# Subtractions moved to VectorE, sums moved into PSUM, gathers and small matmuls issued in another order, in a two-block kernel

## The chip, the cores and the metric

One core of one Trainium2 chip. The metric is device time in microseconds (us), the median of several executions; one more execution was recorded by the hardware profiler, and its views are quoted here. The engines are named as in the profile: PE (TensorE matmul) and PEld (its weight loads), DVE (VectorE), ACT (ScalarE), POOL (GpSimd), SP (SyncE, which here issues most DMAs).

## The reference

512 tokens of width 1024 pass through two blocks. What matters here, cut down:

```
# block 1: attention heads and a 31-tap depthwise convolution side by side
h = a * sigmoid(gate);  h = depthwise_conv(h, 31 taps) + b;  silu(layernorm(h))
# then PEER: 8 heads x 16 experts of 16384 per token
q = x @ wq;  top-k of two halves -> e (expert numbers), g (softmax weights)
h = gelu(x . u[e]);   y = sum_k g*h * v[e]
# block 2: RWKV-7 and NSA attention side by side, gated mix, conv FFN
z = z + (prev - z) * mu                # token shift, prev = z one token earlier
state = state*w + (state@a) b + v k    # 16 heads of 64, in chunks
```

## The kernel before

**Products.** PE multiplies in a fast format that keeps fewer bits, so each matrix is split into a high part (a cast on ACT) and a low part (raw minus high, a subtraction), and each product is three matmuls: hi·hi, lo·hi, hi·lo (`mm3`, L258, recorded at L264 to L266). `Stream` (L208) does that for weights: SP loads a raw tile `wr`, ACT casts `wh` (L245), and POOL subtracts `wl` (L247), or VectorE for the tile numbers in `dve`; for the expert stream `uT` these are tiles 12 to 57.

**Block 1.** `phase1` computes the projections tile by tile, four tiles of convolution channels and attention. `taps` (L346) adds 26 of the 31 taps on VectorE, all but the first with a scalar_tensor_tensor from SBUF tiles into an SBUF accumulator (L353); five are summed on ACT and POOL into `side`, and L355 adds the two. Attention scores go to PSUM banks `pb`, their values to one of two banks `po` for two heads at a time, and `mm` (two banks) takes the projections.

**PEER.** The first 384 tokens are done densely: all 128 tiles of 128 experts (`up`: L821, product with the weights at L832, split at L834 and L835; PE's second product at L861). Of these tiles, 68 are computed ahead, while selection runs (`ahead`), and their `gh` are kept in DRAM. The weights come from one-hot matrices made on VectorE (L774, L777) and multiplied on PE (L782). The last 128 tokens are done by gathers: for each of 128 slots POOL issues an indirect DMA (L796) of the experts' rows `ur` and later `vr`; VectorE reduces `ur` (L805, `slot_up`) and adds `vr` times the result into `acc` (L813, `slot_down`). `v_split` (L673) splits the v tile of each expert tile in halves, of which POOL subtracts one and VectorE the other (L683). The loop from L850 on does one expert tile, one reduction and one update per step; VectorE's and POOL's instructions of a step stand in one queue each.

**Block 2.** `shifted` (L1022) takes a projection from PSUM, multiplies it by the row factors into `z` (L1028), subtracts it from the token before (L1029) and adds `mu` times that (L1030). `Rwkv.pair` (L1481) multiplies the two 64-row halves of a tile on PE (L1486), four column pieces of one half after the other; `front.lower` (L1597) does the same for the chunk matrices (L1603); `invert` works with 32x32 pieces (L1546, L1551, L1553).

**Order.** The engines run their queues in order. A scheduler in the kernel's builder places the instructions of each engine by its own simulation of the program, under the program's dependences and buffer counts; so code that is moved or given to another engine reorders its surroundings too.

## Time and profile before

| | us |
|---|---|
| median of 3 runs (2991.15 to 3003.77) | 2994.53 |
| profiled execution, device time | 2995.58 |
| its span in the profile | 2993.8 |
| busy PE, PEld | 2812.0, 2395.3 |
| busy DVE, ACT, POOL | 2242.7, 1203.3, 1644.9 |

The profile is of one execution. Busy times are unions of an engine's instructions; a line's mean is its mean duration, which for an in-order engine contains the time in which an instruction that has started is held up. "Idle before" is the time in which the engine had nothing running before that group, with what ended it. PE records two instructions for each fp32 matmul. The stages of the span are: up to 300 us block 1's first half, to 773 selection and the tiles ahead, to 1600 the expert loop, to 1930 RWKV's preparation, to 2250 its chunks, then NSA, mixing and FFN.

### The profile page before, as it was taken

What the parts mean: (1) busy time and instruction counts of PE and PEld (TensorE: products, weight loads), DVE (VectorE), ACT (ScalarE), POOL (GpSimd) and SP (SyncE); (2) the same over time, 40 slices, a digit from 0 to 9 for tenths busy, and PEclk for the clock granted to TensorE, in tenths of its full rate; (3) what the DMA queues carried; (4) which work ended last, traced back from release to release, by engine and by line L of the source; (5) the groups of instructions that cost most, each with busy time, mean ns of one, the idle gap of its engine ahead of it and who ended that gap; (6) DMA issues with size and microseconds to landing.
All of it is one profiled execution on the core that took longest, in us unless ns stands there. A gap on an engine that the chain in (4) does not pass through costs nothing. (4 is left out here: it accounts for less than half of the span.)

```text
span 2993.8 us, 42580 instructions
## 1 busy us (share of the span) xinstructions
PE 2812.0 (94%) x15507; PEld 2395.3 (80%) x15507; DVE 2242.7 (75%) x3813; ACT 1203.3 (40%) x2077; POOL 1644.9 (55%) x1157
## 2 busy tenths in 40 slices
PE   7789999998899999999997998999999999999998
PEld 5558899997788888888875786788887877888887
DVE  7984899987689999999996598886336874575611
ACT  4344335676233333333433432211236754444431
POOL 5543340003778888888883476523347745554444
PEclk8779999999999999999998999989999999999999
DMA  3101235676989999999974555544743227233332
GB/s 133 42 15 45 85 120 175 210 275 252 340 304 341 335 331 344 340 324 333 331 277 125 182 165 151 161 145 142 203 143 101 75 64 244 89 99 93 97 93 77
DMA packets 270919, 554.02 MB, mean 185 GB/s; under 512 B 41394, under 2 KB 147890, under 8 KB 268916
## 3 DMA queue, kind: packets, MB, share of 16 engines
q1 hardware_dynamic: 219264, 370.91, 38.5%
q0 software_dynamic: 36864, 134.23, 12.3%
q10 hardware_dynamic: 14580, 46.15, 4.3%
q8 instruction: 122, 2.00, 0.3%
q14 instruction: 89, 0.73, 0.1%
HBM read 464.77 MB, written 83.89 MB: 183 GB/s over the span
## 5 line engine op out<-in xcount | busy, mean ns | idle before, releaser
L247 POOL TENSOR_TENSOR wl<-wr,wh 128x1024 fp32r<-128x1024 f32 x273 | 695.6, 2550 | 538.0 <-ACT wh L245 254.0
L245 ACT CAST wh<-wr 128x1024 fp32r<-128x1024 f32 x319 | 335.3, 1051 | 607.3 <-PE mm L265 163.1
L683 POOL TENSOR_TENSOR vl<-vr,vh 128x512 fp32r<-128x512 f32 x128 | 200.9, 1575 | 244.9 <-ACT vh L682 243.5
L805 DVE CUSTOM_DVE_ANT_0 ur<-ur,hnt 128x1024 f32<-128x1024 f32 x128 | 231.5, 1809 | 44.0 <-DMA ur<-in_u,eix 42.8
L813 DVE SCALAR_TENSOR_TENSOR acc<-vr,hc,acc 128x1024 f32<-128x1024 f32 x128 | 232.5, 1816 | 0.2
L796 POOL DMA_INDIRECT ur<-in_u,eix x128 | 176.6, 1379 | 42.2 <-issue 16.3
L796 POOL DMA_INDIRECT vr<-in_vrow,eix x128 | 156.8, 1225 | 40.3 <-issue 22.1
L861 PE MATMUL pb<-vl,ah 128*128 128x512 f32 x512 | 168.7, 400 | 0.0
L861 PE MATMUL pb<-vh,al 128*128 128x512 f32 x512 | 165.1, 396 | 0.0
L683 DVE TENSOR_TENSOR vl<-vr,vh 128x512 fp32r<-128x512 f32 x128 | 143.7, 1129 | 27.3 <-issue 14.4
L861 PE MATMUL pb<-vh,ah 128*128 128x512 f32 x512 | 162.8, 398 | 0.0
L682 ACT CAST vh<-vr 128x512 fp32r<-128x512 f32 x256 | 144.3, 619 | 31.4 <-DMA vr<-in_vrow 21.3
L353 DVE SCALAR_TENSOR_TENSOR acc<-hp,vecs,acc 128x512 f32<-128x512 f32 x100 | 116.0, 1175 | 0.7
L861 PEld LDWEIGHTS pb<-vl,ah 128*128 128x128 f32 x512 | 97.7, 191 | 23.1
L861 PEld LDWEIGHTS pb<-vh,ah 128*128 128x128 f32 x512 | 97.7, 191 | 22.3
L861 PEld LDWEIGHTS pb<-vh,al 128*128 128x128 f32 x512 | 97.3, 190 | 22.8
L785 ACT ACTIVATE wb<-pb 128x512 f32<-128x512 f32 x96 | 98.2, 1151 | 34.4 <-PE pb L782 33.4
L1944 POOL TENSOR_TENSOR prob<-prob,nz 128x128 f32<-128x128 f32 (+3 forms) x128 | 88.8, 725 | 39.4 <-DVE nz L1941 24.0
L1169 DVE TENSOR_TENSOR tot<-tot,sq 128x512 f32<-128x512 f32 x11 | 17.0, 1548 | 112.9 <-ACT sq L1166 112.9
L861 PE MATMUL po<-vl,ah 128*128 128x512 f32 x256 | 86.5, 402 | 12.2 <-POOL vl L683 8.1
L861 PE MATMUL po<-vh,ah 128*128 128x512 f32 x256 | 85.1, 399 | 12.4 <-ACT ah L834 12.4
L861 PE MATMUL po<-vh,al 128*128 128x512 f32 x256 | 86.3, 402 | 0.0
(1407 smaller groups left out, 8788.4 us busy)
## 6 DMA issues: line engine op xcount, KB each, us to landing
wr<-in_ws SPq DMA_DIRECT2D x191, 512.0 KB
wr<-in_uT SPq DMA_DIRECT2D x128, 512.0 KB
vr<-in_vrow SPq DMA_DIRECT2D x128, 512.0 KB
w_d<-wb ACTq DMA_DIRECT2D x12, 2048.0 KB
wt<-w_d SPq DMA_DIRECT2D x32, 768.0 KB
gh_d<-gh ACTq DMA_DIRECT2D x68, 192.0 KB
gh<-gh_d SPq DMA_DIRECT2D x68, 192.0 KB
rd_d<-z SPq DMA_DIRECT2D x24, 256.0 KB
```

The lines of the kernel that those rows point to most:

```text
L245: c.nc.scalar.copy(h, r)
L247: eng.tensor_sub(lo, r, h)
L353: nc.vector.scalar_tensor_tensor(acc[j], hp[:, tap:tap + S], w[:, tap:tap + 1], acc[j], op0=OP.mult, op1=OP.add)
L682: nc.scalar.copy(h[:, s], r[:, s])
L683: (nc.vector if e % 2 else nc.gpsimd).tensor_sub(lo[:, s], r[:, s], h[:, s])
L785: nc.scalar.activation(wb[:, :, t4:t4 + 4].rearrange("p e t -> p t e"), wp.rearrange("p (t e) -> p t e", t=4), AF.Copy, scale=1.0 / GSCALE)
L796: nc.gpsimd.indirect_dma_start(out=t, out_offset=None, in_=src, in_offset=bass.IndirectOffsetOnAxis(ap=eix[:, s:s + 1], axis=0))
L805: nc.vector.tensor_tensor_reduce(out=u, in0=u, in1=hnt, scale=1.0, scalar=0.0, op0=OP.mult, op1=OP.add, accum_out=hc[:, s:s + 1])
L813: nc.vector.scalar_tensor_tensor(acc, v, ghs[gi][:, s:s + 1], acc, op0=OP.mult, op1=OP.add)
L861: nc.tensor.matmul(outs[i][half], ps[a][:, ts], vs[v][:, half * 512:(half + 1) * 512], start=et == 0 and n == 0, stop=et == NE - 1 and n == 2)
L1169: nc.vector.tensor_add(tot, tot, sq)
L1944: nc.gpsimd.tensor_mul(t, t, z[:, i:i + 1].to_broadcast([P, (i + 1) * P]))
```

## The change

Five edits:

1. `taps` accumulates in a PSUM bank of `po` and writes the SBUF accumulator only in the last addition.
2. `shifted` scales `z` by `1 - mu` on ACT into the projection's own PSUM bank, and one VectorE operation adds `mu` times the token before. The factors `own` are made once.
3. All `v_split` subtractions and all of the `uT` stream from tile 12 on go to VectorE.
4. The first four gathers are issued where the v tiles of the loop's start are split, ahead of the last token tile's one-hots; the reductions of group 0 follow after all tiles ahead; in the loop, the reduction follows `up` as before, from another place in the code.
5. Small matmuls on 64 rows (`pair`, `lower`) and on 32x32 pieces (`invert`) go in turn to two row groups and two banks.

```diff
-                nc.vector.scalar_tensor_tensor(acc[j], hp[:, tap:tap + S], w[:, tap:tap + 1], acc[j], op0=OP.mult, op1=OP.add)
+                nc.vector.scalar_tensor_tensor(ps, hp[:, tap:tap + S], w[:, tap:tap + 1], ps, op0=OP.mult, op1=OP.add)
...
-            nc.vector.tensor_add(acc[j], acc[j], sides[j])
+            nc.vector.tensor_add(acc[j], ps, sides[j])
...
-            (nc.vector if e % 2 else nc.gpsimd).tensor_sub(lo[:, s], r[:, s], h[:, s])
+            nc.vector.tensor_sub(lo[:, s], r[:, s], h[:, s])
...
+            u0 = [gather(c.ins["u"], s, "ur") for s in range(SG)]
...
-        u = gather(c.ins["u"], gi * SG + s, "ur")
+        u = u0[s] if gi == 0 else gather(c.ins["u"], gi * SG + s, "ur")
...
-        slot_up(gi, e)
...
     ahead(NB)
+    for s in range(SG):
+        slot_up(0, s)
...
                 up(gi + 1, e, wts[gi + 1])
+                slot_up(gi + 1, e)
...
-        nc.vector.tensor_mul(z[:, 1:], early.pop(0) if early else proj(), rs)
-        nc.vector.tensor_sub(o, z[:, 0:S], z[:, 1:])
-        nc.vector.scalar_tensor_tensor(o, o, c.vec("mu", n), z[:, 1:], op0=OP.mult, op1=OP.add)
+        ps = early.pop(0) if early else proj()
+        nc.vector.tensor_mul(z[:, 1:], ps, rs)
+
+        nc.scalar.activation(ps, z[:, 1:], AF.Copy, scale=own[:, n:n + 1])
+        nc.vector.scalar_tensor_tensor(o, z[:, 0:S], c.vec("mu", n), ps, op0=OP.mult, op1=OP.add)
...
-            for par in range(2):
-                rows = slice(par * 64, par * 64 + 64)
-                ps = self.bank()
-                for j in range(4):
+            pss = [self.bank() for _ in range(2)]
+            for j in range(4):
+                for par, ps in enumerate(pss):
+                    rows = slice(par * 64, par * 64 + 64)
                     nc.tensor.matmul(ps[:, j * P:(j + 1) * P], lhs[rows, j], rhs[rows, j], start=True, stop=True)
...
-                peer(c, st, Stream(c, [ins["uT"][k] for k in pre_tiles()], dve=range(NTOP, NTOP + NROUTE)), last)
+                peer(c, st, Stream(c, [ins["uT"][k] for k in pre_tiles()], dve=range(NTOP, NE)), last)
```

How the order moves, at three places. First VectorE's queue at the end of the convolution, before (`acc_194` is the fourth channel's accumulator, `mx` and `zs` are softmax maxima and sums):

```order
L435 TENSOR_REDUCE mx_1298<-pb_1294 128x1
L436 TENSOR_TENSOR mx_1274<-mx_1274,hr_1083 128x1
L436 TENSOR_TENSOR mx_1286<-mx_1286,hr_1083 128x1
L353 SCALAR_TENSOR_TENSOR acc_194<-hp_912,vecs,acc_194 128x512
L282 TENSOR_TENSOR hsl_1255<-hn_1236,hsh_1254 128x512
L436 TENSOR_TENSOR mx_1298<-mx_1298,hr_1083 128x1
L439 RECIPROCAL zs_1263<-zs_1263 128x1
L353 SCALAR_TENSOR_TENSOR acc_194<-hp_912,vecs,acc_194 128x512
L439 RECIPROCAL zs_1275<-zs_1275 128x1
L439 RECIPROCAL zs_1287<-zs_1287 128x1
L355 TENSOR_TENSOR acc_194<-acc_194,side_916 128x512
L439 RECIPROCAL zs_1299<-zs_1299 128x1
```

And after (`po_1312` and `po_1392` are the banks of the third and fourth channel; more such rows in turn stand ahead of these):

```order
L355 SCALAR_TENSOR_TENSOR po_1392<-hp_913,vecs,po_1392 128x512
L355 SCALAR_TENSOR_TENSOR po_1312<-hp_666,vecs,po_1312 128x512
L355 SCALAR_TENSOR_TENSOR po_1392<-hp_913,vecs,po_1392 128x512
L357 TENSOR_TENSOR acc_193<-po_1312,side_670 128x512
L355 SCALAR_TENSOR_TENSOR po_1392<-hp_913,vecs,po_1392 128x512 x15
L357 TENSOR_TENSOR acc_194<-po_1392,side_917 128x512
L495 SCALAR_TENSOR_TENSOR acc_191<-mm_1420,acc_191 128x512
L495 SCALAR_TENSOR_TENSOR acc_192<-mm_1420,acc_192 128x512
```

The taps of the last two channels stood among the attention's operations; now some 35 stand together, and the last channel's begin only once the bank of the second pair of heads is read. PE's matmuls on `acc_193` and `acc_194` follow in its queue right behind the last scores.

Second, POOL's queue where the expert loop begins, before (`wl` are weight splits, `ur` and `vr` gathers):

```order
L247 TENSOR_TENSOR wl_7509<-wr_7444,wh_7508 128x1024
L845 MEMSET acc 128x1024
L247 TENSOR_TENSOR wl_7543<-wr_7478,wh_7542 128x1024
L247 TENSOR_TENSOR wl_7577<-wr_7512,wh_7576 128x1024
L247 TENSOR_TENSOR wl_7611<-wr_7546,wh_7610 128x1024
L796 DMA ur_7655<-in_u,eix 128x1024
L796 DMA ur_7665<-in_u,eix 128x1024
L796 DMA ur_7675<-in_u,eix 128x1024
L796 DMA ur_7685<-in_u,eix 128x1024
```

and after:

```order
L248 TENSOR_TENSOR wl_3878<-wr_3813,wh_3877 128x1024
L248 TENSOR_TENSOR wl_3912<-wr_3847,wh_3911 128x1024
L690 DMA ur_6500<-in_u,eix 128x1024
L690 DMA ur_6502<-in_u,eix 128x1024
L690 DMA ur_6504<-in_u,eix 128x1024
L690 DMA ur_6506<-in_u,eix 128x1024
L849 MEMSET acc 128x1024
L690 DMA ur_7715<-in_u,eix 128x1024
L690 DMA vr_7744<-in_vrow,eix 128x1024
L690 DMA ur_7754<-in_u,eix 128x1024
```

The gathers (L690 after, since the helper is moved) stood behind the splits of the last tiles ahead and then in turn with `vl` and `wl` subtractions; now four stand ahead of the clearing of `acc`, and behind it gathers only.

Third, PE's queue at the first of `pair`'s matmuls, before (`kk` and `a` are its operands, `xg` and `wh`, `wl` a projection's):

```order
L265 MATMUL mm_15765<-xg6l,wh_15644 128x512
L266 MATMUL mm_15765<-xg6h,wl_15645 128x512
L1486 MATMUL pb_15352<-kk_15289,a_15286 128x128 x4
L1486 MATMUL pb_15358<-kk_15289,a_15286 128x128 x4
L1443 MATMUL pb_15489<-sqm,tmp_15486 128x2 x4
L264 MATMUL mm_15765<-xg7h,wh_15644 128x512
```

and after (six of the eight, which alternate between two banks):

```order
L266 MATMUL mm_15649<-xg6l,wh_15613 128x512
L267 MATMUL mm_15649<-xg6h,wl_15614 128x512
L1496 MATMUL pb_15358<-kk_15295,a_15292 128x128
L1496 MATMUL pb_15359<-kk_15295,a_15292 128x128
L1496 MATMUL pb_15358<-kk_15295,a_15292 128x128
L1496 MATMUL pb_15359<-kk_15295,a_15292 128x128
L1496 MATMUL pb_15358<-kk_15295,a_15292 128x128
L1496 MATMUL pb_15359<-kk_15295,a_15292 128x128
```

Of the 192 matmuls in `lower` 110 stand singly between matmuls of the other bank; 82 still come in runs of two to four in the same bank. Of `invert`'s 128 at L1546, 64 stand in turn.

## Rows read from the trace of the kernel before

**Rows 1.** The page: busy us (share of the span) xinstructions, whole run.

```profile
PE 2812.0 (94%) x15507; PEld 2395.3 (80%) x15507; DVE 2242.7 (75%) x3813; ACT 1203.3 (40%) x2077; POOL 1644.9 (55%) x1157
```

**Rows 2.** Table by stage: start:end, length, busy us by engine, granted clock, DMA share, GB/s.

```profile
52.00:206.00 154.00, 119.44 (x427) 84.56 (x427) 146.86 (x204) 61.03 (x108) 84.62 (x49) 0.77 0.10 31
...
850.00:1500.00 650.00, 645.72 (x3081) 562.07 (x3080) 611.24 (x638) 233.02 (x438) 557.79 (x354) 1.00 0.94 332
1700.00:1930.00 230.00, 211.58 (x1141) 172.82 (x1142) 209.28 (x238) 63.33 (x108) 156.74 (x103) 0.95 0.53 154
1930.00:2250.00 320.00, 310.27 (x2599) 271.87 (x2598) 171.38 (x341) 71.78 (x123) 120.34 (x103) 0.94 0.52 159
```

**Rows 3.** Groups by line, VectorE, 52 to 206 us: busy us, mean ns, idle before.

```profile
L353 DVE SCALAR_TENSOR_TENSOR acc<-hp,vecs,acc 128x512 f32<-128x512 f32 x92 | 103.3, 1139 | 0.5
L435 DVE TENSOR_REDUCE mx<-pb 128x1 f32<-128x512 f32 x20 | 13.4, 678 | 4.7 <-PE pb L433 4.7
```

**Rows 4.** Timeline, 75 us: start, duration, engine and line.

```profile
74.92 2.59 POOL L247 TENSOR_TENSOR wl<-wr,wh 128x1024 fp32r<-128x1024 f32 x1 [4.24 <-ACT wh L245]
...
75.28 2.77 DVE L355 TENSOR_TENSOR acc<-acc,side 128x512 f32<-128x512 f32 x1
```

**Rows 5.** What PE waited for, 660 to 780 us: total, times, longest.

```profile
PE pb L782 <- DVE og L777: 11.6, 8, 3.3
```

**Rows 6.** One-hots on VectorE: the group, 660 to 730 us.

```profile
L777 DVE TENSOR_TENSOR og<-o,gs 128x1024 f16<-128x1024 f16 x32 | 28.4, 922 | 0.6 <-PE pb L782 0.4
```

**Rows 7.** The same, timeline, 704 us.

```profile
703.93 1.28 DVE L777 TENSOR_TENSOR og<-o,gs 128x1024 f16<-128x1024 f16 x2
```

**Rows 8.** Groups by line, VectorE, whole run: weight splits while POOL rests.

```profile
L247 DVE TENSOR_TENSOR wl<-wr,wh 128x1024 fp32r<-128x1024 f32 x46 | 55.8, 1214 | 9.1 <-ACT wh L245 8.9
```

**Rows 9.** Timeline, 766 to 783 us, POOL's gathers and VectorE.

```profile
766.61 0.94 POOL L796 DMA_INDIRECT ur<-in_u,eix  x1 [0.30 <-issue]
...
770.93 1.23 DVE L805 CUSTOM_DVE_ANT_0 ur<-ur,hnt 128x1024 f32<-128x1024 f32 x1 [41.50 <-DMA ur<-in_u,eix]
...
778.74 1.28 DVE L813 SCALAR_TENSOR_TENSOR acc<-vr,hc,acc 128x1024 f32<-128x1024 f32 x1
...
783.22 1.84 POOL L796 DMA_INDIRECT ur<-in_u,eix  x1 [0.31 <-DVE al L835]
```

**Rows 10.** What PE waited for, 780 to 1600 us.

```profile
PE po L861 <- ACT ah L834: 12.4, 3, 8.0
PE po L861 <- POOL vl L683: 8.1, 11, 2.3
```

**Rows 11.** Groups by line and form, VectorE, 850 to 1500 us.

```profile
L805 DVE CUSTOM_DVE_ANT_0 ur<-ur,hnt 128x1024 f32<-128x1024 f32 x101 | 187.3, 1855 | 1.0 <-DMA ur<-in_u,eix 1.0
L813 DVE SCALAR_TENSOR_TENSOR acc<-vr,hc,acc 128x1024 f32<-128x1024 f32 x102 | 184.3, 1807 | 0.0
L683 DVE TENSOR_TENSOR vl<-vr,vh 128x512 fp32r<-128x512 f32 x101 | 116.4, 1157 | 17.8 <-issue 13.3 <-ACT vh L682 4.3
...
L832 DVE TENSOR_TENSOR mm<-mm,wt 128x384 f32<-128x384 f32 x52 | 28.8, 554 | 4.7 <-ACT mm L830 4.7
```

**Rows 12.** Groups by line, VectorE, 1690 to 1960 us: the token shift.

```profile
L1030 DVE SCALAR_TENSOR_TENSOR z<-z,vecs,z 128x512 f32<-128x512 f32 x20 | 29.3, 1465 | 0.3
L1029 DVE TENSOR_TENSOR z<-z 128x512 f32<-128x512 f32 x20 | 24.5, 1226 | 13.7 <-POOL z L1027 12.8
```

**Rows 13.** Groups by line, PE, 1700 to 2260 us: the small matmuls.

```profile
L1603 PE MATMUL pb<-ar,ck 64*128 64x128 f32 x384 | 51.0, 300 | 0.7 <-ACT X L1617 0.6
...
L1486 PE MATMUL pb<-kk,a 64*128 64x128 f32 x128 | 14.1, 289 | 3.2 <-DVE kk L1480 3.2
...
L1546 PE MATMUL po<-c4y,LT 32*32 32x32 f32 x256 | 9.9, 193 | 0.0
```

**Rows 14.** Timeline, 2050 us: the first and the sixth of a series.

```profile
2049.82 0.19 PE L1553 MATMUL po<-c4y,zz 32*32 32x32 f32 x1
...
2049.90 0.19 PE L1551 MATMUL po<-zz,c4y 32*32 32x32 f32 x1
```

More of the change, by code (lines that the diff above doesn't have):

```diff
@@ L88 @@
 DEC = math.exp(-0.5)
+NMU = 27
 def _tables2():
@@ L349, in taps @@
         for j in range(4):
-            w, hp = c.vec("cdw", j * 31, 31), conv[j]
-            nc.vector.tensor_scalar(acc[j], hp[:, SIDE:SIDE + S], w[:, SIDE:SIDE + 1], None, op0=OP.mult)
+            w, hp, ps = c.vec("cdw", j * 31, 31), conv[j], c.bank("po", 2)
+            nc.vector.tensor_scalar(ps, hp[:, SIDE:SIDE + S], w[:, SIDE:SIDE + 1], None, op0=OP.mult)
             for tap in range(SIDE + 1, 31):
-                nc.vector.scalar_tensor_tensor(acc[j], hp[:, tap:tap + S], w[:, tap:tap + 1], acc[j], op0=OP.mult, op1=OP.add)
+                nc.vector.scalar_tensor_tensor(ps, hp[:, tap:tap + S], w[:, tap:tap + 1], ps, op0=OP.mult, op1=OP.add)
                 yield
-            nc.vector.tensor_add(acc[j], acc[j], sides[j])
+            nc.vector.tensor_add(acc[j], ps, sides[j])
             yield
@@ L544 @@
 NSEL = 4
-NROUTE = NT * NSEL + ND * 10
 TB = 32
@@ L682, in v_split, with gather @@
             nc.scalar.copy(h[:, s], r[:, s])
-            (nc.vector if e % 2 else nc.gpsimd).tensor_sub(lo[:, s], r[:, s], h[:, s])
+            nc.vector.tensor_sub(lo[:, s], r[:, s], h[:, s])
         vsplit[et] = (h, lo)
         v_load(et + VRAW)
+    def gather(src, s, tag):
+        t = c.t4(tag)
+        nc.gpsimd.indirect_dma_start(out=t, out_offset=None, in_=src,
+                                     in_offset=bass.IndirectOffsetOnAxis(ap=eix[:, s:s + 1], axis=0))
+        return t
     for i in order:
@@ L792, in peer @@
     nc.sync.dma_start(hnt, hnt_d)
-    def gather(src, s, tag):
-        t = c.t4(tag)
-        nc.gpsimd.indirect_dma_start(out=t, out_offset=None, in_=src,
-                                     in_offset=bass.IndirectOffsetOnAxis(ap=eix[:, s:s + 1], axis=0))
-        return t
     def slot_up(gi, s):
@@ L1020, in block2 @@
     ntile = [0]
+    own = c.sb.tile([P, NMU], F32, name="own", tag="own", bufs=1)
+    nc.vector.tensor_scalar(own, c.vec("mu", 0, NMU), -1.0, 1.0, op0=OP.mult, op1=OP.add)
     def shifted(o):
@@ L1480, in pair @@
         nc.vector.scalar_tensor_tensor(kk, kk, -1.0, e3, op0=OP.mult, op1=OP.mult)
-        for par in range(2):
-            rows = slice(par * 64, par * 64 + 64)
-            ps = self.bank()
-            for n in range(4):
-                cs = slice(n * P, (n + 1) * P)
+        pss = [self.bank() for _ in range(2)]
+        for n in range(4):
+            cs = slice(n * P, (n + 1) * P)
+            for par, ps in enumerate(pss):
+                rows = slice(par * 64, par * 64 + 64)
                 nc.tensor.matmul(ps[:, cs], a[rows, cs], kk[rows, cs], start=True, stop=True)
+        for par, ps in enumerate(pss):
             nc.vector.tensor_mul(self.LT[g][:, :, par * 4 + j], ps.rearrange("p (n t) -> p n t", n=4),
@@ L1542, in invert @@
                 st.append((u0, pt, q64, c.bank("po", 2), self.sm("zz", [P, 8, 32], bufs=2)))
-            for q0, q1 in quads:
-                for u0, pt, q64, z1, zz in st:
-                    for u in range(8):
+            turns = [[(quads[(a + b) % 2], st[a]) for a in range(2)] for b in range(2)]
+            for turn in turns:
+                for u in range(8):
+                    for (q0, q1), (u0, pt, q64, z1, zz) in turn:
                         nc.tensor.matmul(z1[q1, u * 32:(u + 1) * 32], pt[q0, u, q1], Qc[q0, u0 + u, :], start=True, stop=True)
+                for (q0, q1), (u0, pt, q64, z1, zz) in turn:
                     nc.vector.tensor_copy(zz[q1], z1[q1, 0:256].rearrange("p (u i) -> p u i", u=8))
-            for q0, q1 in quads:
-                for u0, pt, q64, z1, zz in st:
-                    for u in range(8):
+            for turn in turns:
+                for u in range(8):
+                    for (q0, q1), (u0, pt, q64, z1, zz) in turn:
                         nc.tensor.matmul(z1[q1, 256 + u * 32:256 + (u + 1) * 32], Pc[q1, u0 + u, :], zz[q1, u, :],
                                          start=True, stop=True)
+                    for (q0, q1), (u0, pt, q64, z1, zz) in turn:
                         nc.tensor.matmul(z1[q0, 256 + u * 32:256 + (u + 1) * 32], zz[q1, u, :], Pc[q1, u0 + u, :],
                                          start=True, stop=True)
+                for (q0, q1), (u0, pt, q64, z1, zz) in turn:
                     nc.vector.tensor_copy(q64[q1, :, 0:32], z1[q1, 256:512].rearrange("p (u i) -> p u i", u=8))
@@ L1598, in lower @@
             r = []
-            for par in range(2):
-                rows = slice(par * 64, par * 64 + 64)
-                ps = self.bank()
-                for j in range(4):
+            pss = [self.bank() for _ in range(2)]
+            for j in range(4):
+                for par, ps in enumerate(pss):
+                    rows = slice(par * 64, par * 64 + 64)
                     nc.tensor.matmul(ps[:, j * P:(j + 1) * P], lhs[rows, j], rhs[rows, j], start=True, stop=True)
+            for ps in pss:
                 t = self.sm(tag, [P, 4, P], 4 if tag == "rb" else 2)
```

## The prediction

> **What bounds the kernel now.** I read the busy table of the page first. TensorE (PE) is busy for 2812.0 of 2993.8 us, so there are some 180 us in which it does nothing, and whatever the change frees on another engine can be worth only the part of these that it touches [rows 1]. The second view is the table by stage, since the whole-run share hides four different limits. The reader is to see there that in 52 to 206 us (projections, convolution, first attention heads) VectorE is busy for 146.86 of 154 us and PE for 119.44; that the expert loop (850 to 1500) belongs to PE with 645.72 of 650; that in 1700 to 1930 (RWKV preparation) both PE and VectorE are over nine tenths full; and that 1930 to 2250 (RWKV chunks) is PE's with 310.27 of 320 [rows 2]. Third, groups of instructions by line, for what VectorE pays; fourth, the timeline where a duration looks odd; last, what PE waited for.
>
> VectorE's price depends on what GpSimd (POOL) does. A tap takes 1139 ns on average in 52 to 206, although a VectorE operation of the same width that reads PSUM takes 678 [rows 3]. The timeline shows where it comes from: a POOL subtraction starts at 74.92 and runs 2.59 us, and the VectorE addition of two SBUF tiles issued at 75.28 ends with it, after 2.77 us [rows 4]. So three parts of the change attack one thing: two-input SBUF work on VectorE held by POOL arithmetic.
>
> **The change part by part** (against the profiled execution's 2995.58 us; the median of the runs shown is 2994.53, 1 us less).
>
> *Taps into PSUM.* 92 taps lie in the stretch. At 0.68 instead of 1.139 us VectorE gets back 92 x 0.46 = 42 us [rows 3]. PE can use at most its idle 154 - 119 = 35 us [rows 2]. But the order says that not all comes: attention and taps now share the two `po` banks, so the second channel waits while the first scores are done with no tap between, and the last channel can start only when the second pair of heads has left its bank. The last 35 taps stand almost in one piece, with PE's next matmul (the convolution's mean) needing their sum: 35 x 0.68 = 24 us in which PE has nothing, where before the last taps lay between scores. 42 - 24 = 18; attention's own chain is likely to take a third of it, and I take **-12**. Bounds: -35 (PE's idle time gone) and +24 (the tail comes on top of everything as it was).
>
> *Last one-hots.* From 660 to 780 PE waited 11.6 us for the weighted one-hots [rows 5]. The 32 of them take 922 ns each, two undisturbed ones 1.28 us, so POOL holds them for 32 x 0.28 = 9 us, and more on the plain one-hots beside them [rows 6, 7]. With four gathers on POOL there and fewer subtractions, that mostly goes. Against it stand more weight splits on VectorE of 1.21 us each [rows 8], most of them after 730, where VectorE sits idle for 41.5 us [rows 9]. **-6**; bounds -12 and +5.
>
> *Loop start, loop and tail.* From 780 to 1600 PE waited 12.4 us for `ah`, in three waits with one of 8.0, and 8.1 us for `vl` from POOL [rows 10]. The 8.0 us is a queue: the gathers were being issued at 766, behind POOL's subtractions, VectorE idled 41.50 us for the first of them, then had five reductions to do before the products that make `ah` [rows 9]. After, the four gathers are issued before the last one-hots, and POOL holds no subtraction at all, so both waits go: 20 us. What becomes late next is VectorE, which now does all subtractions. Per slot, at undisturbed durations: reduction 1.23 and update 1.28 [rows 9], two `vl` subtractions of half a 1.21 each [rows 8], product and split of the activations 0.55 each, and half a `wl` subtraction (52 of 102 slots compute their projection here) 0.6 [rows 11]: 5.4 us. PE needs 650 / 102 = 6.37 us a slot [rows 2, 11]. The loop stays PE's, with nearly 1 us to spare, and its pace does not change. **-20**; bounds -25 and, if the spare is not there, the slower case below.
>
> The disturbance that is left is the gather itself: its issue takes POOL 0.94 us with VectorE idle and 1.84 us beside VectorE's products [rows 9]. The Trainium skill (page "SBUF — State Buffer", the "DVE blocks DMA" box in "SBUF: two separate sides") warns that VectorE's two-port operations starve the descriptors that GpSimd writes, and its section "Who interferes with whom" infers that tensor_tensor does not; the 1.84 us shows that something is shared here after all. By the warning a denser VectorE would make gathers late. Two of 1.84 are 3.7 us of POOL's 6.37 us slot, so by the rows it stays hidden, and I leave it a part of the slower case.
>
> *Token shift.* 20 of 24 tiles lie in 1690 to 1960: 1226 + 1465 ns for the pair of operations [rows 12]; one with a PSUM input at 0.68 replaces them: 20 x 2.0 = 40 us less on VectorE, out of 209.28 in 230. PE has only 230 - 211.58 = 18 us idle there [rows 2]. ScalarE takes the new scaling (63 of 230 us busy). The `mm` bank is held longer, through multiply, copy and last operation, which often stand side by side in VectorE's queue, so that VectorE waits there for ScalarE, about as long as one PSUM operation. The next projection has the second bank. Of 18 us I take 7. The paired matmuls of this stage (L1486, 14.1 us [rows 13]) now alternate row halves; halved they give 7. **-14**; bounds -25 and +5 (the waits for ScalarE and for the bank eat it all).
>
> *Row halves in the chunks.* L1603 is busy for 51.0 us in 384 records, two to a matmul [rows 13]. In the order after, 110 of its 192 matmuls stand alternately; the others still come in runs, as the scheduler left them. Halving 57% of 51.0 gives 15; half of the 32x32 ones of L1546 (9.9 us) alternate too and give 2. Three quarters of 17, since PE is full there but sits in chains: **-13**. No row shows two row halves side by side; the bounds are 0 and -25. The nearest row: the 32x32 matmuls of L1551 and L1553, which alternate column halves in the same rows, start about 16 ns apart [rows 14], against 9.9 us / 256 = 39 ns for L1546, which stays in one place [rows 13].
>
> The Trainium skill (page "TensorE: Matmul & The Clock Gate", Part 3 "Packing small matmuls") says that a weight load overlaps a running matmul only where the row group differs. By that the alternation would at least halve these matmuls, and L1551 with L1553 should go no faster than L1546; rows 14 shows that they do, so column halves overlap as well and the rule is not the whole story. By the rule alone the two terms would be the same as mine, with the bound of nothing ruled out.
>
> Sum: -12 - 6 - 20 - 14 - 13 = -65, 2930.6 by the profiled execution and **2930** by the median's level. NSA, mixing and FFN keep their order and their time.
>
> **Rivals.**
> 1. *All of it converts.* -35 - 12 - 25 - 25 - 25 = -122: 2873. For it: every wait named is real idle time of PE. Against it: the tail of taps and the small idle time of the RWKV stages.
> 2. *Only the queues' waits go.* Row halves give nothing (+13 + 7 against the forecast) and the taps' tail eats the convolution's gain (+12): 2962. For it: the shared `po` banks, no row of overlapping halves.
> 3. *No change to be measured.* The tail of taps costs its full 24 us instead of gaining 12 (+36) and the row halves give nothing (+20): 2986.
> 4. *Slower: VectorE becomes the loop's bound.* If gathers hold it as the subtractions did, its slot costs what before's contended means say: 1.855 + 1.807 + 2 x 1.157 [rows 11] + 1.1 + 0.6 = 7.7 us; 1.32 us over PE's 6.37 in 124 slots is +164, less the 45 that the other parts give: about 3114. It decides from 6.37 + 45 / 124 = 6.73 us a slot. Against it: reduction and update take 1.23 and 1.28 us at loop start, between gathers [rows 9]; for it: VectorE's queue is in order, and one late gather now holds up all the splits behind it.
>
> **How the numbers follow.** Forecast 0.50 (2905 to 2955), rival 1 0.15, rival 2 0.20, rival 3 0.08, rival 4 0.07. A measurement of this kernel can tell about 0.5%, 15 us, from no change. Faster: 0.50 + 0.15 + 0.20 = 0.85; same 0.08; slower 0.07. The range 2875 to 2975 takes in the forecast, most of rival 2 and half of rival 1, and leaves out some 2 in 10.
>
> **What would show it.** The taps and the last operation of the shift at about 0.68 us, with a block of taps at the end of the convolution in which PE idles some 20 us; no wait of 8 us for `ah` at the loop's start; reduction and update near 1.25 us in the loop and VectorE under 6 us a slot; L1603 well under 51 us. Wrong it would be if the reduction stays near 1.8 us without subtractions on POOL (something else holds VectorE), if PE's share of the loop falls under 0.98, if L1603 keeps its 51 us, or if PE waits for the `mm` bank at each shifted tile.

## The result and the profile after

| | us |
|---|---|
| changed kernel, median of 4 runs (2919.51 to 2922.48) | 2920.9 |
| kernel before, median of 4 runs (2991.15 to 3003.77) | 2997.4 |
| ratio, 95% interval | 0.9741 [0.9713, 0.977] |
| span of the profiled execution, before and after | 2993.8, 2918.8 |

The forecast was 2930. The page's busy line, which answers to [rows 1]: PE is busy 47 us less, VectorE (DVE) 180 and POOL 441 us less.

```profile
PE 2765.1 (95%) x15507; PEld 2367.9 (81%) x15507; DVE 2063.1 (71%) x3985; ACT 1223.2 (42%) x2104; POOL 1203.7 (41%) x959
```

The table by stage, as [rows 2] (start:end, length, busy us of PE, PEld, DVE, ACT, POOL, granted clock, DMA share, GB/s):

```profile
52.00:206.00 154.00, 119.18 (x462) 82.28 (x462) 114.14 (x214) 63.87 (x111) 69.27 (x50) 0.81 0.10 31
850.00:1500.00 650.00, 650.00 (x3150) 574.24 (x3149) 540.83 (x811) 240.48 (x443) 245.90 (x213) 1.00 0.96 340
...
1864.50:2147.70 283.20, 265.42 (x2355) 232.13 (x2354) 166.94 (x319) 65.00 (x113) 105.80 (x90) 0.92 0.53 164
```

In 52 to 206 VectorE falls from 146.86 to 114.14 us while PE stays at 119; in the loop PE has no idle time left and VectorE 109 us. In the chunks (third row, from their first matmul to their last) PE is idle for 18 of 283 us.

Where the 75 us lie is seen best by milestones: the starts of the first and the last instruction of a group, in the one profiled execution of each kernel, and the differences between them. The groups are the weighted-one-hot matmuls, the loop's matmuls `pb<-vh,ah`, the multiplications `z<-mm,rs` of the token shift (the last one alone) and the chunks' matmuls `pb<-ar,ck`. Columns: to the first one-hot matmul; one-hots; to the loop; loop; to the last shifted tile; to the first chunk matmul; chunks; rest; span.

| kernel | to one-hots | one-hots | to loop | loop | shift | pairs | chunks | rest | span |
|---|---|---|---|---|---|---|---|---|---|
| before | 478.9 | 256.2 | 48.3 | 807.6 | 236.4 | 116.0 | 276.0 | 774.4 | 2993.8 |
| changed | 471.3 | 245.1 | 39.2 | 774.3 | 225.8 | 108.8 | 283.2 | 771.1 | 2918.8 |
| u1 taps in SBUF | 478.3 | 245.0 | 43.3 | 772.4 | 225.4 | 112.7 | 270.5 | 774.5 | 2922.1 |
| b1 last channel in SBUF | 474.3 | 245.0 | 39.4 | 774.4 | 226.2 | 109.9 | 272.7 | 778.6 | 2920.5 |
| b3 20 taps a step | 448.1 | 245.1 | 41.1 | 774.5 | 227.4 | 108.7 | 283.3 | 772.5 | 2900.7 |
| c1 20 taps, SBUF | 483.7 | 245.1 | 38.2 | 772.7 | 229.2 | 110.7 | 276.7 | 774.5 | 2930.8 |
| s3 edit 3 alone | 479.9 | 250.5 | 49.2 | 785.3 | 235.2 | 115.5 | 293.7 | 775.0 | 2984.3 |
| u3 edit 3 undone | 470.4 | 243.1 | 49.1 | 833.7 | 229.8 | 113.5 | 265.2 | 773.9 | 2978.7 |
| u4 gathers late | 467.2 | 251.5 | 49.8 | 775.0 | 230.1 | 113.2 | 280.9 | 777.4 | 2945.1 |
| s34 edits 3 and 4 | 483.7 | 245.0 | 37.7 | 772.6 | 235.0 | 117.9 | 278.7 | 770.2 | 2940.8 |
| u2 old shift | 469.7 | 245.0 | 41.1 | 774.5 | 235.2 | 116.1 | 278.4 | 775.8 | 2935.8 |
| u6 64-row order old | 471.6 | 245.1 | 43.3 | 772.8 | 230.4 | 114.5 | 274.9 | 769.6 | 2922.2 |
| u5 inversion order old | 468.1 | 245.0 | 38.3 | 774.8 | 227.6 | 110.9 | 290.2 | 771.3 | 2926.2 |
| c2 20 taps, edit 5 undone | 449.7 | 245.1 | 41.2 | 774.5 | 230.8 | 112.4 | 279.8 | 772.6 | 2906.1 |

From before to changed that is -7.6, -11.1, -9.1, -33.3, -10.6, -7.2, +7.2 and -3.3, together -75.0.

**Convolution.** Groups by line, VectorE, 52 to 206 us of the changed kernel, against [rows 3]; then what PE waited for there:

```profile
L355 DVE SCALAR_TENSOR_TENSOR po<-hp,vecs,po 128x512 f32<-128x512 f32 x89 | 65.1, 751 | 1.0
L437 DVE TENSOR_REDUCE mx<-pb 128x1 f32<-128x512 f32 x24 | 16.3, 687 | 5.9 <-PE pb L435 5.8
```

```profile
PE mm L491 <- DVE acc L357: 26.4, 2, 16.0
PE pb L454 <- ACT pr L440: 5.8, 4, 2.5
```

A tap costs 751 ns instead of 1139, and PE's largest wait is now for the sums of the channels. The timeline at the end shows the block (start, duration, engine, line, count, idle before): 20 taps of two channels and then 15 of one, with PE idle for 16.0 and 10.4 us of them.

```profile
172.79 13.26 DVE L355 SCALAR_TENSOR_TENSOR po<-hp,vecs,po 128x512 f32<-128x512 f32 x20
...
186.56 11.83 DVE L355 SCALAR_TENSOR_TENSOR po<-hp,vecs,po 128x512 f32<-128x512 f32 x15
...
186.70 2.07 PE L491 MATMUL mm<-acc,sqm 128*128 128x512 f32 x2 [16.00 <-DVE acc L357]
199.17 2.07 PE L491 MATMUL mm<-acc,sqm 128*128 128x512 f32 x2 [10.40 <-DVE acc L357]
```

**Loop.** Groups by line and form, VectorE, 850 to 1500 us, against [rows 8, 11], and PE's wait for the activations from 748 to 1600, against [rows 10]:

```profile
L684 DVE TENSOR_TENSOR vl<-vr,vh 128x512 fp32r<-128x512 f32 x212 | 138.2, 687 | 22.8 <-ACT vh L683 20.4 <-issue 1.9
L816 DVE SCALAR_TENSOR_TENSOR acc<-vr,hc,acc 128x1024 f32<-128x1024 f32 x105 | 134.2, 1278 | 0.0
L808 DVE CUSTOM_DVE_ANT_0 ur<-ur,hnt 128x1024 f32<-128x1024 f32 x105 | 128.0, 1219 | 0.0
L248 DVE TENSOR_TENSOR wl<-wr,wh 128x1024 fp32r<-128x1024 f32 x52 | 63.6, 1223 | 17.6 <-ACT wh L246 14.2 <-issue 2.0
```

```profile
PE po L866 <- ACT ah L837: 3.3, 2, 2.4
```

Without arithmetic on POOL the reduction takes 1219 instead of 1855 ns, the update 1278 instead of 1807, a split of `v` 687 instead of 1157; the waits of 12.4 and 8.1 us have become 3.3 and nothing.

### The profile page after: what moved, and what is told of

It is laid out like the page before. It is cut to its first block, busy times and chain, and to the rows that moved or that the text cites. A ratio compares the mean times of both kernels' runs of the same rounds, so it can differ in the third digit from the quotient of the medians.

```text
span 2918.8 us, 42112 instructions
## 1 busy us (share of the span) xinstructions
PE 2765.1 (95%) x15507; PEld 2367.9 (81%) x15507; DVE 2063.1 (71%) x3985; ACT 1223.2 (42%) x2104; POOL 1203.7 (41%) x959
## 4 chain that ended last, share of the span: by engine, by line
PE 59%; DVE 8%; DMA 3%; POOL 1%; issue 1%; ACT 1%; SPq 0%; ACTq 0%; POOLq 0%; DVEq 0%
PE pb L866 11%; PE mm L265 8%; PE mm L267 8%; PE mm L266 8%; PE po L866 6%; PE pb L265 2%; PE pb L267 2%; PE pb L266 2%; PE mm L1981 1%; DVE c4y L1533 1%; PE pb L1620 1%; DVE prob L1955 1%; PE pb L1632 1%; PE po L1806 1%; DVE c4y L1523 1%
## 5 line engine op out<-in xcount | busy, mean ns | idle before, releaser
L248 POOL TENSOR_TENSOR wl<-wr,wh 128x1024 fp32r<-128x1024 f32 x203 | 503.5, 2483 | 433.8 <-ACT wh L246 167.9
L690 POOL DMA_INDIRECT ur<-in_u,eix x128 | 151.1, 1181 | 585.4 <-DVE og L786 184.0
L690 POOL DMA_INDIRECT vr<-in_vrow,eix x128 | 150.3, 1174 | 94.6 <-DVE acc L816 28.1
L684 DVE TENSOR_TENSOR vl<-vr,vh 128x512 fp32r<-128x512 f32 x256 | 167.1, 686 | 23.0 <-ACT vh L683 20.7
L248 DVE TENSOR_TENSOR wl<-wr,wh 128x1024 fp32r<-128x1024 f32 x116 | 141.6, 1221 | 49.2 <-ACT wh L246 45.6
L816 DVE SCALAR_TENSOR_TENSOR acc<-vr,hc,acc 128x1024 f32<-128x1024 f32 x128 | 163.7, 1279 | 0.0
L866 PE MATMUL pb<-vl,ah 128*128 128x512 f32 x512 | 158.1, 390 | 0.0
L866 PE MATMUL pb<-vh,al 128*128 128x512 f32 x512 | 156.0, 389 | 0.0
L808 DVE CUSTOM_DVE_ANT_0 ur<-ur,hnt 128x1024 f32<-128x1024 f32 x128 | 155.8, 1219 | 0.0
L866 PEld LDWEIGHTS pb<-vl,ah 128*128 128x128 f32 x512 | 96.4, 188 | 20.5
L833 ACT ACTIVATE mm<-mm 128x384 f32<-128x384 f32 x60 | 28.5, 475 | 191.6 <-PE mm L267 191.6
L1962 POOL TENSOR_TENSOR prob<-prob,nz 128x128 f32<-128x128 f32 (+3 forms) x128 | 88.8, 725 | 38.3 <-DVE nz L1959 26.6
L1178 DVE TENSOR_TENSOR tot<-tot,sq 128x512 f32<-128x512 f32 x11 | 17.3, 1573 | 112.7 <-ACT sq L1175 112.7
L835 DVE TENSOR_TENSOR mm<-mm,wt 128x384 f32<-128x384 f32 x60 | 33.9, 564 | 66.2 <-ACT mm L833 60.9
```

The costliest lines, as they stand in the source:

```text
L248: eng.tensor_sub(lo, r, h)
L684: nc.vector.tensor_sub(lo[:, s], r[:, s], h[:, s])
L690: nc.gpsimd.indirect_dma_start(out=t, out_offset=None, in_=src, in_offset=bass.IndirectOffsetOnAxis(ap=eix[:, s:s + 1], axis=0))
L808: nc.vector.tensor_tensor_reduce(out=u, in0=u, in1=hnt, scale=1.0, scalar=0.0, op0=OP.mult, op1=OP.add, accum_out=hc[:, s:s + 1])
L816: nc.vector.scalar_tensor_tensor(acc, v, ghs[gi][:, s:s + 1], acc, op0=OP.mult, op1=OP.add)
L866: nc.tensor.matmul(outs[i][half], ps[a][:, ts], vs[v][:, half * 512:(half + 1) * 512], start=et == 0 and n == 0, stop=et == NE - 1 and n == 2)
```

## Experiments

All times are medians of 4 to 10 runs beside the kernel before on the same chip. The runs of one kernel spread by up to 26 us (s3: 2969 to 2995), and the experiments ran on four chips, on which the median of the kernel before was 2987 to 3000 us. So differences between variants of less than about 8 us are read from the stages, not from the totals. The stages are those of one execution each, and that can be an untypical one: in u2 and u4 it is the slowest of four, some 10 us above the median.

**u1: taps back in SBUF.**

```diff
-            w, hp, ps = c.vec("cdw", j * 31, 31), conv[j], c.bank("po", 2)
+            w, hp, ps = c.vec("cdw", j * 31, 31), conv[j], acc[j]
```

> The changed kernel with the convolution taps back in the SBUF accumulator (edit 1 undone). Theory (the block of taps at the convolution's end gives most of VectorE's gain back): in the changed kernel the stretch up to the first one-hot matmul is 7.6 us shorter than before, so undoing costs 5 to 12 us: 2926 to 2933. PE's wait for the channels' sums (26.4 us in two waits in the changed kernel) falls under 3 us, a tap goes from 0.75 to about 1.1 us. Rival (the 42 us of VectorE time are what counts): 2945 to 2960.

Measured: 2921.9, ratio 0.9743 [0.969, 0.9796]. The total is under the theory's range. The stage up to the one-hots is 7 us longer again, as forecast; the total hides it, since the chunk stage came out 13 us shorter (below). PE's waits in 52 to 206 are the old ones again, and only 0.7 us is for the sums:

```profile
PE pb L454 <- ACT pr L440: 12.3, 5, 3.8
PE pb L373 <- ACT hsq L370: 11.5, 1, 11.5
PE pb L433 <- DVE hr L376: 5.3, 1, 5.3
```

**u2: the old token shift.**

```diff
-        nc.scalar.activation(ps, z[:, 1:], AF.Copy, scale=own[:, n:n + 1])
-        nc.vector.scalar_tensor_tensor(o, z[:, 0:S], c.vec("mu", n), ps, op0=OP.mult, op1=OP.add)
+        nc.vector.tensor_sub(o, z[:, 0:S], z[:, 1:])
+        nc.vector.scalar_tensor_tensor(o, o, c.vec("mu", n), z[:, 1:], op0=OP.mult, op1=OP.add)
```

> The changed kernel with the old token shift (edit 2 undone: subtraction and scalar_tensor_tensor on SBUF tiles). Theory (VectorE's load sets the pace between the first shifted tile and the first chunk): the changed kernel is 18 us shorter from the first shifted tile to the first chunk matmul, of which the paired matmuls can be 4 us; undoing costs 10 to 17 us: 2931 to 2938. Rival (the row halves of the paired matmuls do it, VectorE is hidden): 2920 to 2925.

Measured: 2927.5 (2925.8 to 2937.6), ratio 0.9766 [0.9721, 0.9811]: between the two. Its stages point to the theory: shift 235.2 and pairs 116.1, like before (236.4, 116.0), against 225.8 and 108.8. By them edit 2 is worth 17 us; the median of the four runs shows 7, and the profiled execution is the slowest of them (2937.6), so the 17 may be too much.

**u3: edit 3 undone.** The subtractions go back to where they were; the gathers stay early.

```diff
-            nc.vector.tensor_sub(lo[:, s], r[:, s], h[:, s])
+            (nc.vector if e % 2 else nc.gpsimd).tensor_sub(lo[:, s], r[:, s], h[:, s])
...
-                peer(c, st, Stream(c, [ins["uT"][k] for k in pre_tiles()], dve=range(NTOP, NE)), last)
+                peer(c, st, Stream(c, [ins["uT"][k] for k in pre_tiles()], dve=range(NTOP, NTOP + NT * NSEL + ND * 10)), last)
```

> The changed kernel with half of the v subtractions and the uT tiles from 58 on back on POOL (edit 3 undone); the first gathers stay early. Theory (POOL's arithmetic holds VectorE's two-input operations, and both are late for PE in places, each wait followed by a stretch at the lower clock): the loop, 774 us in the changed kernel, takes 795 to 807 again and the time is 2940 to 2955; the reduction goes back from 1.22 to about 1.8 us. Rival (the early gathers bring the loop's gain, since the one wait of 8 us at its start is the largest): 2920 to 2926.

Measured: 2981.5, ratio 0.995 [0.9931, 0.9969], worse than either forecast: the loop takes 833.7 us, 26 more than before. The reduction is held again (VectorE, 850 to 1500), and PE waits for splits all through the loop:

```profile
L808 DVE CUSTOM_DVE_ANT_0 ur<-ur,hnt 128x1024 f32<-128x1024 f32 x101 | 193.1, 1912 | 0.0
```

```profile
PE po L866 <- POOL vl L684: 26.6, 20, 4.9
PE po L866 <- ACT vh L683: 5.4, 5, 1.1
PE po L866 <- DVE vl L684: 4.9, 3, 3.1
```

**s3: edit 3 alone, on the kernel before.** Same two lines, the other way round.

> The kernel before with edit 3 alone: all v subtractions and all uT subtractions from tile 12 on go to VectorE. Theory (the subtractions on POOL are what made the loop slow, through VectorE operations held by them and through splits that POOL finished late; undoing edit 3 in the changed kernel cost 60 us): the loop, 808 us before, takes 775 to 785, the one-hots win their 11 us, 2945 to 2957. Rival (edit 3 pays only together with the early gathers and the new place of the reductions): 2965 to 2985.

Measured: 2981.9 (2969 to 2995), ratio 0.9951 [0.9917, 0.9984]. The rival had the total right. The stages say why: the one-hots and the loop gain 28 us, nothing is gained at the loop's start, and 18 us are lost in the chunks, whose code edit 3 does not touch: PE's idle time there is that of the kernel before (9.8 and 9.7 us), but the granted clock is 0.88 instead of 0.95. At the start VectorE now waits for the one-hot weights:

```profile
772.38 0.57 DVE L832 TENSOR_TENSOR mm<-mm,wt 128x384 f32<-128x384 f32 x1 [17.77 <-DMA wt<-w_d]
```

**u4: the gathers late, POOL without subtractions.**

```diff
-            u0 = [gather(c.ins["u"], s, "ur") for s in range(SG)]
...
-        u = u0[s] if gi == 0 else gather(c.ins["u"], gi * SG + s, "ur")
+        u = gather(c.ins["u"], gi * SG + s, "ur")
```

> The changed kernel with the first four gathers issued where their reductions stand, after all tiles ahead (edit 4 undone in its main part), POOL still without subtractions. Theory (what delayed the gathers before was POOL's queue of subtractions, and that is gone): they are late by little, the wait for the first activations stays under 5 us, 2921 to 2927. Rival (the place of issue is what counts): the wait of 8 us and the cold stretch behind it come back, 2930 to 2937.

Measured: 2938.0, ratio 0.9793 [0.9744, 0.9841]: 1 us over the rival's range. The place of issue does count, but the wait is another one. PE's waits for the activations are the first row; POOL, which has nothing else to do, issues 13 gathers between the second row and the third, while SyncE issues the loop's own loads; and VectorE's first product of the loop waits 18 us for `wt` (fourth row), until 761, where the changed kernel had it by 752:

```profile
PE po L865 <- ACT ah L836: 23.9, 3, 20.5
```

```profile
730.26 1.20 POOL L690 DMA_INDIRECT ur<-in_u,eix  x1 [14.30 <-DMA wr<-in_uT]
...
750.54 0.94 POOL L690 DMA_INDIRECT ur<-in_u,eix  x1 [0.30 <-issue]
```

```profile
761.24 0.57 DVE L834 TENSOR_TENSOR mm<-mm,wt 128x384 f32<-128x384 f32 x1 [18.04 <-DMA wt<-w_d]
```

In [rows 9] the start waited for gathers stuck behind subtractions. With the subtractions gone it waits for a transfer in place of a queue. From the first issue of a `wt` load to that product 32 us pass here, with 13 gathers beside it, and 26 in the changed kernel, with 8; the DMA engines are full in both stretches (share 1.05 and 1.07). That the gathers take the load's share is argued from this, not shown.

**s34: edits 3 and 4 together, without 1, 2 and 5.**

> Edits 3 and 4 together without 1, 2 and 5 (taps in SBUF, old token shift, old order of the small matmuls). Edit 3 alone gave 10 us, edit 4 without 3 (with 1, 2 and 5) some 15 over before. Theory (the two need each other: without subtractions POOL sends a burst of 13 gathers ahead of the weights that the loop's start waits for, and without the move of the subtractions the early gathers only feed the same queue): the loop starts by 770 instead of 783 and takes about 774 us, 2935 to 2948. Rival (the parts just add, and the rest of the 75 us lies in edits 1, 2 and 5): 2960 to 2975.

Measured: 2945.8, ratio 0.9828 [0.9786, 0.9871], as the theory said. From the first one-hot to the loop's end the four combinations are: neither 1112.1 us, edit 3 alone 1085.0, edit 4 without 3 1125.9 (u3), both 1055.3. So edit 4 costs 14 us without edit 3 and gives 30 beside it. (u3 has edits 1, 2 and 5 as well; with edits 3 and 4 both in place those three change this stretch by 3 us, from 1055.3 to 1058.6.)

**u5 and u6: the old orders of the small matmuls.** u5 restores the loops of the inversion, u6 (below, `lower`; `pair` likewise) the 64-row ones.

```diff
-            for j in range(4):
-                for par, ps in enumerate(pss):
-                    rows = slice(par * 64, par * 64 + 64)
+            for par, ps in enumerate(pss):
+                rows = slice(par * 64, par * 64 + 64)
+                for j in range(4):
```

> The changed kernel with the 32x32 matmuls of the inversion in their old order (part of edit 5 undone). Theory (in the changed kernel PE waits 16.5 us before L1559, 9.3 of it for the evacuation of the first product, since both quarters' products now end together and their evacuations follow one another): those waits fall under 6 us, the chunk stage goes from 283 to about 272 us, 2908 to 2915. Rival (the waits come from where the scheduler put the inversions, not from their inner order): 2917 to 2926, the waits stay over 10 us.

> The changed kernel with the 64-row matmuls of the pairs and of the chunk matrices in their old order, one row half after the other (part of edit 5 undone). Theory (two row halves in turn run at about 59 ns a record instead of 96, and PE sets the pace in the chunks): their busy time goes from 42.5 + 10.3 back to about 51 + 14 us, the time is 2928 to 2937. Rival (the gain is lost in waits of the chunk chains): 2917 to 2925.

Measured: u5 2926.6, ratio 0.9779 [0.9706, 0.9853]; u6 2924.4, ratio 0.976 [0.969, 0.9831]. Both theories fell; u6 lies in its rival's range, u5 a little over its rival's. PE's groups by line over the whole run, of u5 and then of u6:

```profile
L1558 PE MATMUL po<-c4y,LT 32*32 32x32 f32 x256 | 11.0, 203 | 7.5 <-DMA c4y<-t_d 4.4 <-DVE zz L1559 3.1
```

```profile
L1620 PE MATMUL pb<-ar,ck 64*128 64x128 f32 x384 | 48.1, 293 | 0.4 <-ACT U L1682 0.4
...
L1496 PE MATMUL pb<-kk,a 64*128 64x128 f32 x128 | 13.7, 285 | 2.8 <-DVE Y L1535 2.7
```

In u5 the waits before L1558 fell from 16.5 to 7.5 us, and the chunks still took 290 us, 7 more. In u6 the busy time came back (48.1 and 13.7 us against 42.5 and 10.3), the shift and pair stages lost 10 us together, and the chunks were 8 us shorter.

**b1: the last channel in SBUF**, to tell whether the banks make the block of taps.

```diff
-            w, hp, ps = c.vec("cdw", j * 31, 31), conv[j], c.bank("po", 2)
+            w, hp, ps = c.vec("cdw", j * 31, 31), conv[j], c.bank("po", 2) if j < 3 else acc[j]
```

> The changed kernel with the last of the four convolution channels accumulated in SBUF again, the other three in PSUM, so that this channel need not wait for a bank. Theory (the block of taps at the end, 26.4 us of PE waits, exists because two channels' taps can start only when the second pair of heads has left its bank): PE's wait for the sums falls to 8 to 16 us, the first one-hot matmul comes 6 to 14 us earlier, 2908 to 2916. Rival (the taps of that channel, now at 1.1 us and in the attention's way, cost what the block saves): 2917 to 2925.

Measured: 2924.0, ratio 0.976 [0.969, 0.9831]: the theory fell. The last channel needs no bank, and its 25 taps stand at the end all the same; PE waits 28.9 us for the sums:

```profile
171.99 7.88 DVE L355 SCALAR_TENSOR_TENSOR po<-hp,vecs,po 128x512 f32<-128x512 f32 x10
...
181.03 19.65 DVE L355 SCALAR_TENSOR_TENSOR acc<-hp,vecs,acc 128x512 f32<-128x512 f32 x25
200.71 0.69 DVE L357 TENSOR_TENSOR acc<-acc,side 128x512 f32<-128x512 f32 x1
```

**b3: 20 taps a step.** The program advances the taps by `TAPS` at each of five attention steps and then issues what is left in one go, ahead of the convolution's norm: of 4 x 26 steps of the generator, 60 with 12 a step, 100 with 20.

```diff
-TAPS = 12
+TAPS = 20
```

> The changed kernel with TAPS = 20 instead of 12: the generator of the convolution's taps is advanced by 20 taps at each attention step, so that few are left behind the fourth (with 12 it is 44, which the code issues in one go). In VectorE's order the last piece without attention operations shrinks from 35 taps to 5. Theory (after b1 the bank is out; the block at the end is the 44 taps that the program itself puts behind the fourth head, since 12 a step was set for taps of 1.1 us): PE's wait for the channels' sums falls from 26 to under 8 us, the first one-hot comes 8 to 18 us earlier, 2903 to 2914. Rival (taps placed earlier delay the attention chain by as much): 2917 to 2926.

Measured: **2902.1** (2900.7 to 2904.4), ratio 0.968 [0.9639, 0.9722], the fastest of all. PE's waits in 52 to 206, against those of the changed kernel above:

```profile
PE pb L454 <- ACT pr L440: 6.4, 4, 3.1
PE mm L491 <- DVE acc L357: 5.8, 1, 5.8
```

The first one-hot comes 23 us earlier than in the changed kernel; the wait that went was 20.6.

**c1: 20 taps a step, but in SBUF.** u1 and b3 combined.

> 20 taps a step as in the run before (2902 us), but accumulated in SBUF as in the kernel before. Theory (what the PSUM accumulator gives is VectorE's time, and the place of the taps in the program lets PE have it): taps are held by POOL again at over 1 us each, stand in the attention's way, and the time is 2915 to 2932, no better than the changed kernel or that kernel with SBUF taps (2922). Rival (the number of taps a step is all, the accumulator's place does nothing): 2899 to 2908.

Measured: 2931.7, ratio 0.9787 [0.9725, 0.9849], as the theory said. The taps are held again (VectorE, 52 to 206), and PE waits for the attention's chain (52 to 215):

```profile
L355 DVE SCALAR_TENSOR_TENSOR acc<-hp,vecs,acc 128x512 f32<-128x512 f32 x91 | 102.6, 1144 | 0.5
```

```profile
PE pb L454 <- ACT pr L440: 13.4, 5, 6.3
PE pb L373 <- ACT hsq L370: 11.5, 1, 11.5
...
PE mm L491 <- DVE acc L357: 0.7, 1, 0.7
```

**c2: 20 taps a step, edit 5 undone.** b3, u5 and u6 combined.

> 20 taps a step with all small matmuls in their old order (edit 5 undone; taps in PSUM, edits 2 to 4 as in the changed kernel). Theory (edit 5 saves PE some 15 us of busy time, but the chunk stage's length follows the scheduler's order of the chains: 265 to 294 us in kernels that share its code): the time stays within 8 us of 2902. Rival (edit 5 gives what its busy time says): 2912 to 2920.

Measured: 2907.0 (2905.9 to 2909.5), ratio 0.9713 [0.9652, 0.9774], within the 8 us of the theory. It is 4.9 us over b3, but on another chip, and the intervals of the two ratios overlap, so the totals do not settle what edit 5 is worth. By the stages shift and pairs are 7 us longer than in b3 and the chunks 3.5 shorter: a few us in all, less than the 13.6 us of busy time that the edit saves (below).

## Why the prediction was right, and where not

**Taps, -12 forecast, -7.6 measured.** Right in size: VectorE got its time (751 ns, a little over the 678 taken), and the tail of some 35 taps cost PE 26.4 us where 24 were forecast. The reason given for the tail was wrong. The prediction put it down to the `po` banks; b1 takes the last channel's bank away and the tail stays, b3 leaves the banks and it goes. It hangs on the program's own order: 12 taps a step left 44 behind the fourth head. That alone does not make the tail, for u1 has the same 12 a step with SBUF taps, and PE waits there for the attention's chain, only 0.7 us for the sums. c1 shows the other half: without the PSUM accumulator 20 taps a step give no gain. The tail also cost more than its length, which the sum had left out: around it the granted clock was 0.51, nearly all of the time at the lower of the two levels (1.2 GHz), and in b3 it was 0.80 over the same times:

```profile
158.00:220.00 62.00, 29.35 (x76) 18.52 (x76) 46.13 (x73) 12.20 (x19) 2.43 (x3) 0.51 0.00 0
```

**One-hots, -6 forecast, -11.1 measured.** The prediction named both causes, fewer subtractions on POOL and the gathers there, and took half of the size. Edit 3 alone gives half (s3: 250.5; u4, without the early gathers, 251.5). The early gathers give all of it even without edit 3 (u3: 243.1), as the two do together (245.0).

**Loop, -20 forecast, -42.4 measured** (start 9.1, loop 33.3): the term that was mis-sized. The step that failed is that a wait costs its own length, and that the pace does not change. The waits inside the loop were 16.5 us (20.5 in [rows 10] and 4.0 for one late split on VectorE, less the 8.0 ahead of the loop); 2.4 of such waits are left. At the loop's start, behind the wait of 8.0 us, and at its end, where waits of 2.3 and 4.0 us stand, PE ran below its full clock, as these rows of the kernel before show (17 us at a granted clock of 0.86, 92 us at 0.96, which is 6 us):

```profile
783.00:800.00 17.00, 17.00 (x70) 14.17 (x69) 16.11 (x17) 4.50 (x9) 15.38 (x10) 0.86 0.93 335
1500.00:1592.00 92.00, 84.11 (x371) 69.98 (x370) 71.44 (x71) 24.75 (x48) 63.76 (x41) 0.96 0.63 217
```

In the changed kernel both ends of the loop run at 1.00 (755.6 to 772 and 1440 to 1530); 772 to 850 at 0.98 costs 1.6 us, like 800 to 850 at 0.97 before. That is 20 of the 33 us. Most of the rest is PE's pace itself, at a granted clock of 1.00 from 850 to 1500 in both kernels: the loop's matmul records have medians of 392 to 396 ns before and 389 after (six groups, 2304 records), which is 10 us. One of the groups, of the kernel before, of s3 and of u4 (minimum, median, maximum, first and last start):

```profile
L861 PE MATMUL pb<-vh,ah x512: 390/395/628, 783.4 to 1591.0; 128*128 128x512 f32 x171
L861 PE MATMUL pb<-vh,ah x512: 390/393/628, 779.6 to 1564.9; 128*128 128x512 f32 x171
L865 PE MATMUL pb<-vh,ah x512: 389/389/628, 768.5 to 1543.5; 128*128 128x512 f32 x171
```

The long records stay with edit 3 alone (s3). They are gone in every kernel with the reductions in their new place, also with the gathers issued late (u4); only one of the six groups of u3 still has 393. So this part, some 10 us of loop (785.3 in s3, 775.0 in u4), goes with the part of edit 4 that the prediction gave no price, the move of the reductions; why PE then runs the same matmuls faster is left open. Some 3 us are left without a cause. That VectorE would bear the load was right: 540.8 of 650 us, 1.22 and 1.28 us for reduction and update; rival 4 is out. And the cause given for the wait at the start, POOL's queue, was only the first of two: in u4 and s3, without that queue, the start waits for the loads of `wt`.

**Token shift and pairs, -14 forecast, -17.8 measured.** VectorE's last operation takes 744 ns and waits 12.1 us in all for ScalarE's scaling, as forecast, and PE had the second bank: from 1590 to 1870 it waited for this operation once, 3.9 us. The split of the term does not hold: 7 us were taken for the paired matmuls, whose busy time fell by 3.8 (14.1 to 10.3), and what u2 and u6 lose in these two stages, 17 and 10 us, is more than the 17.8 that both edits gave, so the two effects overlap.

```profile
L1039 DVE SCALAR_TENSOR_TENSOR z<-z,vecs,mm 128x512 f32<-128x512 f32 x22 | 16.4, 744 | 13.0 <-ACT mm L1038 12.1 <-issue 0.8
```

**Chunks, -13 forecast, +7.2 measured.** The sign failed, and two steps behind it. The first is the size of the overlap: the term halved the alternating matmuls. The nearest row that it had, 16 against 39 ns, flattered: undisturbed, L1546's records start 32 ns apart. The row halves do overlap, but what they save is less than half: 16 records of the paired matmuls took 1.71 us before and 1.16 after, that is, less the last one's 0.27, (1.16 - 0.27) / 15 = 59 ns a record instead of 96:

```profile
1722.01 1.71 PE L1486 MATMUL pb<-kk,a 64*128 64x128 f32 x16
```

```profile
1651.01 1.16 PE L1496 MATMUL pb<-kk,a 64*128 64x128 f32 x16
```

The Trainium skill (page "TensorE: Matmul & The Clock Gate", Part 3 "Packing small matmuls") gives 3.07 times for four row tiles; two row halves gave 96 / 59 = 1.6 times here, so the trace agrees in kind.

The three groups in the chunks and pairs lost 13.6 us of busy time (42.5, 10.3 and 8.6 against [rows 13]) where halving gave 24:

```profile
L1620 PE MATMUL pb<-ar,ck 64*128 64x128 f32 x384 | 42.5, 308 | 0.0
...
L1496 PE MATMUL pb<-kk,a 64*128 64x128 f32 x128 | 10.3, 303 | 3.1 <-DVE Y L1535 3.1
L1559 PE MATMUL po<-c4y,LT 32*32 32x32 f32 x256 | 8.6, 209 | 16.5 <-DVE zz L1561 9.3 <-DMA c4y<-t_d 7.2
```

The second step is that this stage's length was taken as PE's work alone, at an unchanged clock and with no new wait. The chunks before, to be held against the third row of the table by stage above:

```profile
1943.40:2219.40 276.00, 266.27 (x2308) 233.76 (x2308) 158.37 (x317) 63.39 (x111) 97.77 (x82) 0.95 0.54 166
```

Busy time times granted clock is, as an estimate, PE's work at full clock: 253 us before and 244 after. So the work did fall by 9 us. But the granted clock fell from 0.95 to 0.92, which costs 8 us more than before, and PE was idle for 17.8 instead of 9.7 us; 12.3 of these are two waits ahead of L1559, for the evacuation before it and for a DMA. Together that is the 7 us. (47 more matmul records fall into the changed kernel's stretch, so its work is rather over- than understated.)

The stage ranges from 265 to 294 us over kernels most of which have the same code there. In part that is the scheduler: b1 and the changed kernel differ in one line of block 1, their matmuls stand in another order in the chunks, and they differ there by 10 us. In part it is the clock: u1, c1 and u3 have almost the same order of PE's matmuls and the same idle time within 1.5 us, and still differ by up to 11.5 us:

```profile
1877.10:2147.60 270.50, 262.41 (x2308) 228.24 (x2307) 158.81 (x317) 64.43 (x112) 102.16 (x82) 0.93 0.55 170
1879.60:2156.30 276.70, 268.21 (x2308) 233.28 (x2307) 158.86 (x317) 64.12 (x112) 102.17 (x82) 0.91 0.53 166
1939.60:2204.80 265.20, 255.72 (x2307) 220.88 (x2307) 159.39 (x317) 64.22 (x112) 102.10 (x82) 0.96 0.56 173
```

The sign of this term is therefore not edit 5's alone. Which placements are good, and what sets the clock there, is left open.

**Rest, 0 forecast, -3.3 measured.** Within what the kernels show with the same code there (769.6 to 778.6).

Altogether -65 was forecast and -75 found: the loop gained 22 us more than its term, the chunks 20 less than theirs. That these two errors nearly cancel is luck, and the sum is closer than its parts deserve.

## What to carry to other kernels

In this kernel VectorE, whose two-input SBUF operations were held by POOL's arithmetic, got faster by taking that arithmetic over; the condition to work out first is that its sum at undisturbed prices stays under the bounding engine's pace (5.4 against 6.37 us a slot here). When an operation gets cheaper, look for the constants in the program that were set for its old price: 12 taps a step took back 23 of the 31 us by which the cheaper taps could bring the one-hots forward. And two edits around one queue are to be tried together: edits 3 and 4 gave 57 us from the first one-hot to the loop's end, edit 3 alone 27, edit 4 without it -14. Where a stage's length hangs on the granted clock and on the order that a scheduler finds, a difference of 10 us in it is no evidence for an edit made elsewhere.
